# Transformer block on one core: the order of key-value root, key transposes and query sums around the last Strassen pair

## The chip, the cores and the metric

One core of a Trainium2 chip runs the whole program. The metric is device time in microseconds, the median of three runs. The core has five engines, each with its own instruction queue that it works through in order: PE (TensorE: matmuls and transposes), DVE (VectorE), ACT (ScalarE), POOL (GpSimd) and SP (SyncE, which here only issues DMAs). They meet through semaphores.

## The reference, cut to what matters

The layer is a residual block: a recurrent branch and a latent attention branch, mixed by gates, then a mixture of experts. Only the latent attention's entrance matters here. 1024 tokens, width 1024, query latents of 768, key-value latents of 256, 16 heads:

```
proj = u @ w_in                       # u = rms_norm(h); holds q_c, kv_c, k_pe among others
q  = (rms_norm(q_c, q_a_g) @ w_uq)    # 768 -> 16 heads x 96
kv = (rms_norm(kv_c, kv_a_g) @ w_ukv) # 256 -> 16 heads x (64 + 64): k_nope, v
k  = concat(k_nope, k_pe)             # k_pe, 32 wide, is the same for all heads
q  = rms_norm(q, q_norm_g); k = rms_norm(k, k_norm_g)
rope on the last 32 of q and k; chunk-causal softmax(q k^T / sqrt(96)) v
```

The norms of the latents need, for each token, the sum of squares over all features of the latent, and one over its root. The kernel applies that factor late, to values, to the sums of keys and queries, and divides the rotated key part by it.

## The kernel before, in words

Tokens lie along the free dimension in the projection: a latent tile is 128 features by 1024 tokens. Weights and activations are split into a high and a low part and multiplied three times, so that the result is near full precision. `pair(c0, ...)` (L227) computes two feature tiles by one level of Strassen: 7 products of 12 matmuls with 512 columns each, 84 in all. Its two weight tiles come through the raw tiles s0, s1, s2 in turn (`raw_tile`).

The stage in question runs in this order as written: the pair of the key-value latents (`latents(C_KV)`), their scaled high and low parts ckh and ckl (L620, L621), the rotation of the shared key part (L623 to L629), the last pair, which is the fifth and sixth tile of the query latents (`latents(C_Q + 4 * P)`), then the key-value sums over features (`token_sums(sk)`: 8 matmuls against a column of ones into pss), the root (`inverse`: L614 and the small DVE operations L80 to L92, into rkv), its reciprocal and its product with kpeR (L633, L634), the scaled query latents written to c_d (L636, L637), eight transposes of kpeR (ptk, L642), and the sums and root of the query latents (ss4, rq). After that comes `keys` (L705) and `values` (L764) for eight pairs of heads, two by two with the weights ukv of a group, while ACT and DVE split the query latents read back from c_d into cqh and cql (L1057, L96).

The order on each engine is not the order of the text. The program is written for a framework that places instructions in each engine's queue by when its own model has them ready, and keeps a tile's reuse safe by waits. Tiles of a pool come free when their last reader is done; the region of the activations (pool up) is released behind the last pair, and the tiles s9 and above lie in it, c_d's readings among them.

```
h = 0; r.append(raw_tile()...); nc.sync.dma_start(r[h], w_in_v[...])   # pair: weights
pss[:, i:i+1] = sq[:, i*P:(i+1)*P].T @ ones[:, :1]                      # token_sums, 8 times
st = raw_tile(); nc.sync.dma_start(st, w_ukv[...]); split(wh, wl, st)    # load_ukv
```

Of the kernel before, what the change touches and what calls it, by code (L numbers as in the profile page):

```python
# [10 lines left out]
F32 = mybir.dt.float32  # L11
# [3 lines left out]
AF = mybir.ActivationFunctionType  # L15
OP = mybir.AluOpType
# [3 lines left out]
P = 128  # L20
T = 1024
D = 1024
NT = T // P
KD = D // P
QL, KVL = 768, 256
# [5 lines left out]
EPS = 1e-6  # L31
# [7 lines left out]
def block_kernel(ctx: ExitStack, tc, a, out):  # L39
    nc = tc.nc  # L40
# [32 lines left out]
    def rsqrt(dst, src, shape, pool):  # L73

        n = int(np.prod(shape))
        view = lambda t: t if len(shape) == 1 else t.rearrange("p (a b) -> p a b", a=shape[0])
        gi = pool.tile([P, n], I32, tag=f"rsi{n}", name="rs_i")
        tt = pool.tile([P, n], F32, tag=f"rst{n}", name="rs_t")
        g3, t, y = view(gi), view(tt), view(gi.bitcast(F32))
        V.tensor_scalar(g3, src.bitcast(I32), 1, -1, op0=OP.arith_shift_right, op1=OP.bitwise_xor)  # L80
        V.tensor_tensor(gi, gi, magic[:, :n], op=OP.add)
        if n == 1:
            hs = pool.tile([P, 1], F32, tag="rsh", name="rs_h")
            V.tensor_scalar(hs, src, -0.5, None, op0=OP.mult)
            for it in range(3):
                V.scalar_tensor_tensor(t, y, y, hs, op0=OP.mult, op1=OP.mult)
                V.scalar_tensor_tensor(dst if it == 2 else y, t, 1.5, y, op0=OP.add, op1=OP.mult)
            return
        for it in range(3):
            V.tensor_tensor(t, y, y, op=OP.mult)  # L90
            V.scalar_tensor_tensor(t, t, -0.5, src, op0=OP.mult, op1=OP.mult)
            V.scalar_tensor_tensor(dst if it == 2 else y, t, 1.5, y, op0=OP.add, op1=OP.mult)  # L92
# [32 lines left out]
    def bank(nm="ps"):  # L125
        return bank2(nm)[:, 0] if psA is None else psA.tile([P, 512], F32, tag="ps", name=nm)
# [299 lines left out]
    def col(nm, k):  # L426
        return pcol[:, rows[nm] + k:rows[nm] + k + 1]
# [41 lines left out]
        V.tensor_scalar(hbx, pcol[:, rows["lru_bx"]:rows["lru_bx"] + 8], 0.5, None, op0=OP.mult)  # L469


    def token_sums(sq):

        pss = bank("pss")
        for i in range(NT):
            TE.matmul(pss[:, i:i + 1], sq[:, i * P:(i + 1) * P], ones[:, :1], start=True, stop=True)
        return pss[:, :NT]
# [119 lines left out]
    lk = tc.alloc_tile_pool(name="lk", bufs=1, side="right", reuse_waits="tile")  # L597
    ckh = lk.tile([P, 2, T], F32R, name="ckh")
    ckl = lk.tile([P, 2, T], F32R, name="ckl")
    with tc.tile_pool(name="wB", bufs=2, side="right", reuse_waits="tile") as wB:  # L600

        def latents(c0):
            t = wB.tile([P, 2, T], F32, tag="o", name="o")
            o = [t[:, j] for j in range(2)]
            pair(c0, o, S.copy)
            sacc, sq = (wB.tile([P, T], F32, tag=nm, name=nm, bufs=1) for nm in ("sacc", "sq"))
            S.activation(sacc, o[0], AF.Square)
            S.activation(sq, o[1], AF.Square)
            V.tensor_tensor(sacc, sacc, sq, op=OP.add)
            return o, sacc  # L610

        def inverse(dst, pss, n):
            sr = wB.tile([P, NT], F32, tag="sr", name="sr")
            V.tensor_scalar(sr, pss, 1.0 / n, EPS, op0=OP.mult, op1=OP.add)  # L614
            rsqrt(dst, sr, [NT], wB)

        o, sk = latents(C_KV)
        for j in range(2):
            g1 = col("kv_a_g", j)
            S.activation(ckh[:, j], o[j], AF.Copy, scale=g1)  # L620
            V.scalar_tensor_tensor(ckl[:, j], o[j], g1, ckh[:, j].bitcast(F32), op0=OP.mult, op1=OP.subtract)  # L621
        ksq = wB.tile([P, NT, DR], F32, name="ksq", bufs=1)
        S.activation(ksq, kp, AF.Square)  # L623
        V.tensor_reduce(sspe, ksq, axis=AX.X, op=OP.add)
        t1 = wB.tile([P, NT, DR], F32, name="t1", bufs=1)
        V.tensor_tensor(kpeR, kp, tC[:, 1], op=OP.mult)
        V.tensor_tensor(t1[:, :, :16], kp[:, :, 16:], tS[:, 1, :, :16], op=OP.mult)
        V.tensor_tensor(t1[:, :, 16:], kp[:, :, :16], tS[:, 1, :, 16:], op=OP.mult)
        V.tensor_tensor(kpeR, kpeR, t1, op=OP.add)  # L629
        oq, sq_ = latents(C_Q + 4 * P)  # L630
        inverse(rkv, token_sums(sk), KVL)
        rec = wB.tile([P, NT], F32, name="rec", bufs=1)
        V.reciprocal(rec, rkv)  # L633
        V.tensor_tensor(kpeR, kpeR, rec.unsqueeze(2).to_broadcast([P, NT, DR]), op=OP.mult)  # L634
        for j in range(2):
            S.activation(oq[j], oq[j], AF.Copy, scale=col("q_a_g", 4 + j))  # L636
            nc.gpsimd.dma_start(c_d[(4 + j) * P:(5 + j) * P, :], oq[j])  # L637
        kpT = wB.tile([P, T], F32, tag="sq", name="kpT", bufs=1)
        for hf in range(2):
            pt = bank("ptk").rearrange("p (c t) -> p c t", c=4)  # L640
            for i in range(4):
                TE.transpose(pt[:DR, i], kpeR[:, 4 * hf + i], ident)  # L642
            V.tensor_copy(kpT[:DR, hf * 512:(hf + 1) * 512].rearrange("p (i t) -> p i t", i=4), pt[:DR])
        nc.gpsimd.dma_start(pe_d, kpT[:DR])
        V.tensor_tensor(ss4, ss4, token_sums(sq_), op=OP.add)
        inverse(rq, ss4, QL)
    up.release()
    psA.release()
    psA = None
# [23 lines left out]
    def side_bank(nm):  # L673
        return psW.tile([P, 2, 512], F32, tag="po", name=nm, bufs=1)
# [22 lines left out]
    def keys(pp, wC):  # L697

        wh, wl = ukv[pp // 2]
        c = slice(pp % 2 * P, pp % 2 * P + P)  # L700
        ps = bank2("pk")
        for hf in range(2):
            for k in range(2):
                for n, (l, r) in enumerate(((wh, ckh), (wh, ckl), (wl, ckh))):
                    TE.matmul(ps[:, hf], l[:, 0, k, c], r[:, k, hf * 512:(hf + 1) * 512],  # L705
                              start=(k == 0 and n == 0), stop=(k == 1 and n == 2))
        ps = ps.rearrange("p h t -> p (h t)")
        kt = wC.tile([P, T], F32, tag="kt", name="kt")
        sq = new(17 + pp)
        S.activation(sq, ps, AF.Square)  # L710
        S.activation(kt, ps, AF.Copy, scale=col("k_norm_g", 0))
        nc.gpsimd.dma_start(k_d[pp * P:(pp + 1) * P, :], kt)
        sqs.append(sq)
        run_late()
        if pp % 4 == 3:
            late.append(lambda: sums(pp // 4))
# [343 lines left out]
    with tc.tile_pool(name="wC", bufs=2, side="right", reuse_waits="tile") as wC:  # L1060
        for g in range(4):
            keys(2 * g, wC)
            if g < 3:
                ukv[g + 1] = load_ukv(g + 1)
            else:
                uq[0] = load_uq(0)
            values(g, 0, wC)
            keys(2 * g + 1, wC)
            values(g, 1, wC)
# [524 lines left out]
```

## Time and profile before

| | |
|---|---|
| median of three runs | 1420.1 us (1417.18 to 1422.19) |
| profiled execution, its own time | 1418.82 us |
| its span, first to last instruction | 1417.1 us |
| mean granted clock of PE, share of full | 0.979 |
| busy PE, DVE, ACT, POOL | 1344.1, 1090.0, 783.0, 382.0 us |
| chain that ended last | PE 83%, DVE 11%, DMA 2%, ACT 2% |

All times below are microseconds from the span's start in the profiled execution. A row of a timeline gives start, duration, engine, line and operation, and in brackets how long the engine had been idle before and what released it. PEclk is the granted clock as a share of 2.4 GHz; 0.5 is 1.2 GHz.

### The profile page before, as it was taken

The numbers are of one execution on the slowest core, as the hardware profiler recorded it, in microseconds if no ns is written. First come the engines' busy times: TensorE is split into PE (matmuls) and PEld (weight loads), VectorE is DVE, ScalarE is ACT, GpSimd is POOL, SyncE is SP. The second block draws the span as 40 slices with busy tenths as digits, with TensorE's granted clock in tenths as the row PEclk, the third lists the DMA queues.
The fourth block names the chain that finished last, engine by engine and source line by source line (L and its number), as shares of the span: only waits on it lengthen the run. The fifth ranks groups of instructions, "written<-read, shape, count | busy, mean of one in ns | idle before, by whom it ended". The sixth has DMA issues, their size and how long they took to land.

```text
span 1417.1 us, 20382 instructions
## 1 busy us (share of the span) xinstructions
PE 1344.1 (95%) x7371; PEld 1094.3 (77%) x7372; DVE 1090.0 (77%) x1894; ACT 783.0 (55%) x1138; POOL 382.0 (27%) x313
## 2 busy tenths in 40 slices
PE   5999999999999899998999999998995999999995
PEld 4967888888888788987655555557874999999995
DVE  7698878787966655678577777785496899999894
ACT  5444747565734353423444444444532888888884
POOL 2100000000000211221777777550422222222222
PEclk9999999999999899999999999999997999999998
DMA  6112222222353545643434444363567899999962
GB/s 216 49 59 87 89 75 89 75 90 89 134 178 120 178 173 172 174 148 99 116 100 117 107 120 132 107 220 134 198 233 250 289 379 381 380 380 379 368 175 36
DMA packets 119945, 244.32 MB, mean 172 GB/s; under 512 B 32636, under 2 KB 68564, under 8 KB 119840
## 3 DMA queue, kind: packets, MB, share of 16 engines
q1 hardware_dynamic: 101768, 194.37, 40.9%
q0 software_dynamic: 17616, 48.46, 11.1%
q8 instruction: 59, 0.97, 0.3%
q14 instruction: 46, 0.38, 0.1%
q10 hardware_dynamic: 456, 0.14, 0.0%
HBM read 203.87 MB, written 55.83 MB: 183 GB/s over the span
## 4 chain that ended last, share of the span: by engine, by line
PE 83%; DVE 11%; DMA 2%; ACT 2%; issue 1%; POOL 0%; SPq 0%; POOLq 0%; DVEq 0%; ACTq 0%
PE pw L245 22%; PE pg L1442 13%; PE po L971 6%; PE py L1479 6%; PE pq L787 6%; PE ph L1172 4%; PE psm L923 3%; PE psl L560 3%; PE pss L953 3%; PE pss L955 2%; PE pss L954 2%; PE pt L1424 2%; PE pp L164 2%; PE pk L705 2%; PE pv L764 1%; DVE s L96 1%
## 5 line engine op out<-in xcount | busy, mean ns | idle before, releaser
L96 ACT CAST s<-s 128x1024 fp32r<-128x1024 f32 (+4 forms) x392 | 337.9, 882 | 179.8 <-PE pw L245 39.7
L96 DVE TENSOR_TENSOR s<-s,s 128x1024 fp32r<-128x1024 f32 (+3 forms) x384 | 382.5, 1023 | 52.8 <-ACT s L96 47.4
L1442 PE MATMUL pg<-s,s 128*128 128x256 f32 x1536 | 196.3, 284 | 0.7 <-DVE s L96 0.7
L1442 PEld LDWEIGHTS pg<-s,s 128*128 128x128 f32 x1536 | 189.8, 191 | 3.5 <-DVE s L96 0.9
L245 PE MATMUL pw<-uh,s 128*128 128x512 f32 x576 | 183.0, 392 | 0.0
L956 ACT ACTIVATE s<-pss 128x512 f32<-128x512 f32 (+4 forms) x192 | 90.1, 493 | 148.6 <-PE pss L955 144.9
L976 POOL TENSOR_TENSOR s<-s,s 128x896 f32<-128x896 f32 (+6 forms) x108 | 149.8, 1406 | 58.3 <-ACT s L956 40.8
L245 PEld LDWEIGHTS pw<-uh,s 128*128 128x128 f32 x576 | 108.8, 189 | 23.9 <-ACT s L96 0.9
L924 DVE TENSOR_REDUCE mx<-psm 128x1 f32<-128x320 f32 (+4 forms) x192 | 94.5, 547 | 41.1 <-PE psm L923 40.7
L245 PE MATMUL pw<-ul,s 128*128 128x512 f32 x288 | 112.7, 391 | 0.0
L971 PE MATMUL po<-s,s 128*64 128x512 f32 (+3 forms) x384 | 106.8, 507 | 0.3 <-ACT s L956 0.3
L1172 PE MATMUL ph<-s,s 128*128 128x512 f32 x384 | 98.3, 404 | 3.5 <-ACT s L96 2.9
L787 PE MATMUL pq<-s,cqh 128*128 128x384 f32 x384 | 99.2, 337 | 0.0
L1479 PE MATMUL py<-s,hT 128*128 128x512 f32 x384 | 96.2, 399 | 1.2 <-ACT hT L96 1.2
L1485 POOL DMA_INDIRECT out_dram<-s,idx x32 | 54.7, 1709 | 121.6 <-ACT s L1484 107.4
L1172 PEld LDWEIGHTS ph<-s,s 128*128 128x128 f32 x384 | 70.6, 191 | 19.5 <-ACT s L96 4.1
L1479 PEld LDWEIGHTS py<-s,hT 128*128 128x128 f32 x384 | 69.8, 188 | 15.1 <-ACT hT L96 1.4
L953 PE MATMUL pss<-s,s 128*128 128x512 f32 (+4 forms) x192 | 72.9, 380 | 3.0 <-ACT s L956 3.0
L1416 POOL DMA_INDIRECT s<-xs,idx x32 | 35.7, 1117 | 131.2 <-PE pt L1424 107.1
L953 PEld LDWEIGHTS pss<-s,s 128*128 128x128 f32 x192 | 36.4, 189 | 44.0 <-DVE mx L924 17.0
L787 PEld LDWEIGHTS pq<-s,cqh 128*128 128x128 f32 x384 | 69.2, 188 | 1.1 <-DVE vt L768 0.8
L955 PE MATMUL pss<-s,s 128*128 128x512 f32 (+4 forms) x192 | 65.8, 343 | 0.0
(389 smaller groups left out, 2603.8 us busy)
## 6 DMA issues: line engine op xcount, KB each, us to landing
s<-in_w_gate_dram SPq DMA_DIRECT2D x64, 512.0 KB
s<-in_w_up_dram SPq DMA_DIRECT2D x63, 512.0 KB
s<-in_w_down_dram SPq DMA_DIRECT2D x63, 512.0 KB
s<-in_w_in_dram SPq DMA_DIRECT2D x40, 512.0 KB
s<-rk_d SPq DMA_DIRECT2D x16, 384.0 KB
q_d<-qt POOLq DMA_DIRECT2D x8, 768.0 KB, 4.7
s<-q_d SPq DMA_DIRECT2D x16, 384.0 KB
s<-in_w_uq_dram SPq DMA_DIRECT2D x12, 384.0 KB
```

The source lines that it names most:

```text
L96: return S.copy(hi, src), by.tensor_tensor(lo, src, hi.bitcast(F32), op=OP.subtract)
L245: TE.matmul(ps[at], w[:, l, k], ub[b][m][:, k], start=(go and k == 0 and n == 0), stop=(k == K4 - 1 and n == 2), skip_group_check=True)
L787: TE.matmul(p2[:, t % 2, :384], l[:, k, i * P:(i + 1) * P], wq[k // 2][r][:, k % 2], start=(k == 0 and n == 0), stop=(k == 5 and n == 2))
L924: V.tensor_reduce((mx[:, j, R1 + i:R1 + i + 1], mx2[:, j, i:i + 1])[b], ps[:, :cn], axis=AX.X, op=OP.max, negate=True)
L953: TE.matmul(o[:, :cn], kh[:, ks], qh[:, q], start=True, stop=False)
L955: TE.matmul(o[:, :cn], kh[:, ks], ql[:, q], start=False, stop=True)
L956: S.activation(pT[:, b * cn:(b + 1) * cn], o[:, :cn], AF.Exp)
L971: TE.matmul(po[pp][s][j * DV:(j + 1) * DV, lo - s * 512:], va[:, c, j, :], pTs[j][:, lo - c * P:hi - c * P], start=(c == 0), stop=(c == 4 ...
L976: (V if pp == NP - 1 and j == 0 and c < 5 else G).tensor_tensor(ac, ac, pTs[j][:, :T - c * P], op=OP.add)
L1172: TE.matmul(o, m2[l][:, k], wo[c][k // 2][r][:, k % 2], start=(k == 0 and m == 0), stop=(k == KD - 1 and m == 2))
L1442: TE.matmul(pg[:, u], l[:, k], r, start=(k == 0 and m == 0), stop=(k == KD - 1 and m == 2))
L1479: TE.matmul(py[hf], l[:, k, :], wd[k][w][:, hf * 512:(hf + 1) * 512], start=(k == 0 and m == 0), stop=(k == 1 and m == 2))
```

## The change

`inverse` is moved out of the stage's pool and takes a pool as an argument. The key-value sums, the root, the product with kpeR, the eight transposes and the write to pe_d are now written ahead of the last pair. The sums of squares of the two pairs no longer share a tile: the key-value ones get a tile of their own (sk), the query ones a raw tile (saq). The sums and the root of the query latents are written into the loop over keys and values, behind `keys(0)`, with a side bank of PSUM as their target.

```
--- before.py
+++ after.py
@@ -469,9 +469,9 @@
         V.tensor_scalar(hbx, pcol[:, rows["lru_bx"]:rows["lru_bx"] + 8], 0.5, None, op0=OP.mult)
 
 
-    def token_sums(sq):
-
-        pss = bank("pss")
+    def token_sums(sq, pss=None):
+
+        pss = bank("pss") if pss is None else pss
         for i in range(NT):
             TE.matmul(pss[:, i:i + 1], sq[:, i * P:(i + 1) * P], ones[:, :1], start=True, stop=True)
         return pss[:, :NT]
@@ -597,24 +597,25 @@
     lk = tc.alloc_tile_pool(name="lk", bufs=1, side="right", reuse_waits="tile")
     ckh = lk.tile([P, 2, T], F32R, name="ckh")
     ckl = lk.tile([P, 2, T], F32R, name="ckl")
+
+    def inverse(dst, pss, n, pool):
+        sr = pool.tile([P, NT], F32, tag="sr", name="sr")
+        V.tensor_scalar(sr, pss, 1.0 / n, EPS, op0=OP.mult, op1=OP.add)
+        rsqrt(dst, sr, [NT], pool)
+
     with tc.tile_pool(name="wB", bufs=2, side="right", reuse_waits="tile") as wB:
 
-        def latents(c0):
+        def latents(c0, sums):
             t = wB.tile([P, 2, T], F32, tag="o", name="o")
             o = [t[:, j] for j in range(2)]
             pair(c0, o, S.copy)
-            sacc, sq = (wB.tile([P, T], F32, tag=nm, name=nm, bufs=1) for nm in ("sacc", "sq"))
+            sacc, sq = sums(), wB.tile([P, T], F32, tag="sq", name="sq", bufs=1)
             S.activation(sacc, o[0], AF.Square)
             S.activation(sq, o[1], AF.Square)
             V.tensor_tensor(sacc, sacc, sq, op=OP.add)
             return o, sacc
 
-        def inverse(dst, pss, n):
-            sr = wB.tile([P, NT], F32, tag="sr", name="sr")
-            V.tensor_scalar(sr, pss, 1.0 / n, EPS, op0=OP.mult, op1=OP.add)
-            rsqrt(dst, sr, [NT], wB)
-
-        o, sk = latents(C_KV)
+        o, sk = latents(C_KV, lambda: wB.tile([P, T], F32, name="sk", bufs=1))
         for j in range(2):
             g1 = col("kv_a_g", j)
             S.activation(ckh[:, j], o[j], AF.Copy, scale=g1)
@@ -627,14 +628,10 @@
         V.tensor_tensor(t1[:, :, :16], kp[:, :, 16:], tS[:, 1, :, :16], op=OP.mult)
         V.tensor_tensor(t1[:, :, 16:], kp[:, :, :16], tS[:, 1, :, 16:], op=OP.mult)
         V.tensor_tensor(kpeR, kpeR, t1, op=OP.add)
-        oq, sq_ = latents(C_Q + 4 * P)
-        inverse(rkv, token_sums(sk), KVL)
+        inverse(rkv, token_sums(sk), KVL, wB)
         rec = wB.tile([P, NT], F32, name="rec", bufs=1)
         V.reciprocal(rec, rkv)
         V.tensor_tensor(kpeR, kpeR, rec.unsqueeze(2).to_broadcast([P, NT, DR]), op=OP.mult)
-        for j in range(2):
-            S.activation(oq[j], oq[j], AF.Copy, scale=col("q_a_g", 4 + j))
-            nc.gpsimd.dma_start(c_d[(4 + j) * P:(5 + j) * P, :], oq[j])
         kpT = wB.tile([P, T], F32, tag="sq", name="kpT", bufs=1)
         for hf in range(2):
             pt = bank("ptk").rearrange("p (c t) -> p c t", c=4)
@@ -642,8 +639,10 @@
                 TE.transpose(pt[:DR, i], kpeR[:, 4 * hf + i], ident)
             V.tensor_copy(kpT[:DR, hf * 512:(hf + 1) * 512].rearrange("p (i t) -> p i t", i=4), pt[:DR])
         nc.gpsimd.dma_start(pe_d, kpT[:DR])
-        V.tensor_tensor(ss4, ss4, token_sums(sq_), op=OP.add)
-        inverse(rq, ss4, QL)
+        oq, saq = latents(C_Q + 4 * P, raw_tile)
+        for j in range(2):
+            S.activation(oq[j], oq[j], AF.Copy, scale=col("q_a_g", 4 + j))
+            nc.gpsimd.dma_start(c_d[(4 + j) * P:(5 + j) * P, :], oq[j])
     up.release()
     psA.release()
     psA = None
@@ -1060,6 +1059,9 @@
     with tc.tile_pool(name="wC", bufs=2, side="right", reuse_waits="tile") as wC:
         for g in range(4):
             keys(2 * g, wC)
+            if g == 0:
+                V.tensor_tensor(ss4, ss4, token_sums(saq, side_bank("pss")[:, 0]), op=OP.add)
+                inverse(rq, ss4, QL, wC)
             if g < 3:
                 ukv[g + 1] = load_ukv(g + 1)
             else:
```

On PE, between the two pairs, before: pw_3647 is the last product of the key-value pair, pw_3757 the first of the last pair (uh, ul: high and low part of the activations; s: weight tiles).

```order
L245 MATMUL pw_3647<-ul1_115,s5_3713 128x512
L245 MATMUL pw_3647<-uh1_113,s5_3713 128x512
L245 MATMUL pw_3757<-uh0_112,s6_3754 128x512
L245 MATMUL pw_3757<-ul0_114,s6_3754 128x512
L245 MATMUL pw_3757<-uh0_112,s6_3754 128x512 x2
L245 MATMUL pw_3757<-ul0_114,s6_3754 128x512
```

The last pair follows the key-value pair directly. The same place in the changed kernel (pw_3798 is now the first product of the last pair, pss the key-value sums, ptk the transposes):

```order
L245 MATMUL pw_3647<-ul1_115,s5_3713 128x512
L245 MATMUL pw_3647<-uh1_113,s5_3713 128x512
L476 MATMUL pss_3746<-ones_80,sk_3729 128x1 x8
L639 MATMUL ptk_3774<-ident_72,kpeR_710 32x128 x4
L639 MATMUL ptk_3780<-ident_72,kpeR_710 32x128 x4
L245 MATMUL pw_3798<-uh0_112,s6_3795 128x512
L245 MATMUL pw_3798<-ul0_114,s6_3795 128x512
```

The sums and the transposes have moved in front of all matmuls of the last pair. On PE behind the last pair, before (pk: keys, sacc: the sums of squares of the two pairs):

```order
L245 MATMUL pw_3791<-uh1_113,s7_3857 128x512
L476 MATMUL pss_3878<-ones_80,sacc_3729 128x1 x8
L642 MATMUL ptk_3910<-ident_72,kpeR_710 32x128 x4
L642 MATMUL ptk_3916<-ident_72,kpeR_710 32x128 x4
L476 MATMUL pss_3923<-ones_80,sacc_3873 128x1 x8
L705 MATMUL pk_4074<-ckh_3597,s3_4041 128x512
L705 MATMUL pk_4074<-ckl_3598,s3_4041 128x512
L705 MATMUL pk_4074<-ckh_3597,s8_4042 128x512
```

Behind the last product stand key-value sums, transposes, query sums and then the keys. The same place in the changed kernel (s1 holds the sums of squares of the query latents, s3 and s8 the weights ukv of group 0, high and low, pv the values):

```order
L245 MATMUL pw_3832<-uh1_113,s7_3898 128x512
L476 MATMUL pss_4067<-ones_80,s1_3914 128x1 x8
L704 MATMUL pk_4049<-ckh_3597,s3_4016 128x512
L704 MATMUL pk_4049<-ckl_3598,s3_4016 128x512
L763 MATMUL pv_4101<-s3_4016,ckh_3597 128x256
L704 MATMUL pk_4131<-ckh_3597,s3_4016 128x512
L704 MATMUL pk_4049<-ckh_3597,s8_4017 128x512
L704 MATMUL pk_4049<-ckh_3597,s3_4016 128x512
```

Only the query sums are left there, still ahead of the first key matmul; four matmuls that don't need s8 come next. On SP around the first reading of c_d, before (s0, s1: raw tiles for ukv, s11 and above: query latents):

```order
L678 DMA s1_4092<-in_w_ukv_dram 128x2x512
L678 DMA s0_4039<-in_w_ukv_dram 128x2x512
L678 DMA s0_4198<-in_w_ukv_dram 128x2x512
L678 DMA s1_4313<-in_w_ukv_dram 128x2x512
L1057 DMA s11_4047<-c_d_70 128x1024
L1057 DMA s12_4051<-c_d_70 128x1024
L1057 DMA s13_4055<-c_d_70 128x1024
L1057 DMA s14_4059<-c_d_70 128x1024
L1057 DMA s16_4067<-c_d_70 128x1024
L1057 DMA s15_4063<-c_d_70 128x1024
```

All four ukv loads are issued ahead of the c_d readings; s0_4039 is the one of group 0. In the changed kernel:

```order
L677 DMA s0_4092<-in_w_ukv_dram 128x2x512
L677 DMA s0_4313<-in_w_ukv_dram 128x2x512
L1056 DMA s11_4022<-c_d_70 128x1024
L1056 DMA s12_4026<-c_d_70 128x1024
L1056 DMA s13_4030<-c_d_70 128x1024
L677 DMA s1_4014<-in_w_ukv_dram 128x2x512
L1056 DMA s14_4034<-c_d_70 128x1024
L1056 DMA s15_4038<-c_d_70 128x1024
L1056 DMA s16_4042<-c_d_70 128x1024
L677 DMA s1_4198<-in_w_ukv_dram 128x2x512
```

The load of group 0 (s1_4014, in the tile that holds the query sums of squares) now stands behind three c_d readings, that of group 2 behind all six.

In DVE's queue the low part of group 0's weights, s8, was made in the course of the last pair; now it stands behind the root of the query latents and two of the six splits cql.

## Rows read from the trace of the kernel before

**Rows 1.** The page's chain that ended last, share of the span by engine

```profile
PE 83%; DVE 11%; DMA 2%; ACT 2%; issue 1%; POOL 0%; SPq 0%; POOLq 0%; DVEq 0%; ACTq 0%
```

**Rows 2.** PE in order of time, 480 to 494 (start us, us, operation)

```profile
480.19 1.84 PE L476 MATMUL pss<-ones,sacc 128*128 128x1 f32 x16
...
487.99 1.89 PE L642 MATMUL ptk<-ident,kpeR 128*32 128x128 f32 x8 [5.97 <-DVE kpeR L634]
...
489.67 3.41 PE L476 MATMUL pss<-ones,sacc 128*128 128x1 f32 x16
...
492.95 0.77 PE L705 MATMUL pk<-ckh,s 128*128 128x512 f32 x1
```

**Rows 3.** Stretches (us, busy by engine, PEclk, DMA share, GB/s)

```profile
482.10:487.95 5.85, 0.00 (x0) 0.00 (x0) 5.50 (x17) 2.17 (x2) 2.15 (x3) 0.58 0.95 366
...
493.05:496.70 3.65, 3.65 (x10) 2.88 (x10) 2.17 (x13) 0.00 (x0) 0.00 (x0) 0.50 0.60 197
...
505.50:546.00 40.50, 40.50 (x270) 34.09 (x270) 19.99 (x42) 19.22 (x21) 9.70 (x15) 1.00 0.66 232
```

**Rows 4.** PE inside the keys

```profile
505.48 0.39 PE L764 MATMUL pv<-s,ckh 128*128 128x256 f32 x1 [1.23 <-ACT kt L711]
```

**Rows 5.** DVE in order of time, 461 to 467

```profile
461.35 0.69 DVE L272 TENSOR_TENSOR o<-pw,o 128x512 f32<-128x512 f32 x1 [1.33 <-PE pw L245]
...
463.22 1.23 DVE L609 TENSOR_TENSOR sacc<-sacc,sq 128x1024 f32<-128x1024 f32 x1
...
466.76 0.68 DVE L268 TENSOR_TENSOR s<-s,s 128x512 f32<-128x512 f32 x1
```

**Rows 6.** DVE in order of time, 482 to 485

```profile
482.06 0.17 DVE L614 TENSOR_SCALAR sr<-pss 128x8 f32<-128x8 f32 x1 [0.98 <-PE pss L476]
...
482.75 1.00 DVE L80 TENSOR_SCALAR rs_i<-sr 128x8 int32<-128x8 int32 x1
...
484.54 1.22 DVE L609 TENSOR_TENSOR sacc<-sacc,sq 128x1024 f32<-128x1024 f32 x1
```

**Rows 7.** POOL in order of time, at three places

```profile
468.59 1.98 POOL L844 TENSOR_SCALAR_AFFINE_SELECT s<-s 128x512 f32<-128x512 f32 x3
...
482.32 1.42 POOL L851 TENSOR_SCALAR_AFFINE_SELECT s<-s 128x1024 f32<-128x1024 f32 x1
...
635.86 2.38 POOL L887 TENSOR_TENSOR s<-s,s 96x1024 f32<-96x1024 f32 x1 [0.36 <-DMA s<-pe_d]
```

**Rows 8.** DVE at 636

```profile
636.10 2.18 DVE L92 SCALAR_TENSOR_TENSOR rs_i<-rs_t,rs_i 128x32 f32<-128x32 f32 x1
```

**Rows 9.** DVE in order of time, behind the last pair

```profile
480.39 0.69 DVE L272 TENSOR_TENSOR o<-pw,o 128x512 f32<-128x512 f32 x1 [2.03 <-PE pw L245]
...
493.12 0.16 DVE L645 TENSOR_TENSOR ss<-ss,pss 128x8 f32<-128x8 f32 x1 [2.52 <-PE pss L476]
...
493.52 0.17 DVE L80 TENSOR_SCALAR rs_i<-sr 128x8 int32<-128x8 int32 x1
...
499.70 6.91 DVE L96 TENSOR_TENSOR cql<-s,cqh 128x1024 fp32r<-128x1024 f32 x6 [4.00 <-ACT cqh L96]
```

**Rows 10.** PE in order of time, 664 to 668

```profile
664.25 0.77 PE L953 MATMUL pss<-s,s 128*128 128x512 f32 x1 [3.00 <-ACT s L956]
...
667.37 0.39 PE L954 MATMUL pss<-s,s 128*128 128x512 f32 x1
```

**Rows 11.** ACT in order of time

```profile
472.50 2.19 ACT L96 CAST s<-s 128x512 fp32r<-128x512 f32 x4 [4.40 <-DMA s<-in_w_ukv_dram]
...
482.06 1.06 ACT L607 ACTIVATE sacc<-o 128x1024 f32<-128x1024 f32 x1 [0.34 <-PE pss L476]
```

**Rows 12.** The queue of SP, an earlier ukv load

```profile
468.85 0.37 SPq L678 DMA_DIRECT2D s<-in_w_ukv_dram  x1
```

**Rows 13.** DMA issues, 440 to 512 (count, size, us to landing)

```profile
c_d<-o POOLq DMA_DIRECT2D x2, 512.0 KB, 6.9
```

More of the change, by code (lines that the diff above doesn't have):

```diff
@@ L469, in decay_consts, with token_sums @@
         V.tensor_scalar(hbx, pcol[:, rows["lru_bx"]:rows["lru_bx"] + 8], 0.5, None, op0=OP.mult)
-    def token_sums(sq):
-        pss = bank("pss")
+    def token_sums(sq, pss=None):
+        pss = bank("pss") if pss is None else pss
         for i in range(NT):
@@ L599, in block_kernel, with inverse, latents @@
     ckl = lk.tile([P, 2, T], F32R, name="ckl")
+    def inverse(dst, pss, n, pool):
+        sr = pool.tile([P, NT], F32, tag="sr", name="sr")
+        V.tensor_scalar(sr, pss, 1.0 / n, EPS, op0=OP.mult, op1=OP.add)
+        rsqrt(dst, sr, [NT], pool)
     with tc.tile_pool(name="wB", bufs=2, side="right", reuse_waits="tile") as wB:
-        def latents(c0):
+        def latents(c0, sums):
             t = wB.tile([P, 2, T], F32, tag="o", name="o")
@@ L605, in latents @@
             pair(c0, o, S.copy)
-            sacc, sq = (wB.tile([P, T], F32, tag=nm, name=nm, bufs=1) for nm in ("sacc", "sq"))
+            sacc, sq = sums(), wB.tile([P, T], F32, tag="sq", name="sq", bufs=1)
             S.activation(sacc, o[0], AF.Square)
@@ L610, in latents @@
             return o, sacc
[L612 to L617, printed above, removed]
+        o, sk = latents(C_KV, lambda: wB.tile([P, T], F32, name="sk", bufs=1))
         for j in range(2):
@@ L629, in block_kernel @@
         V.tensor_tensor(kpeR, kpeR, t1, op=OP.add)
-        oq, sq_ = latents(C_Q + 4 * P)
-        inverse(rkv, token_sums(sk), KVL)
+        inverse(rkv, token_sums(sk), KVL, wB)
         rec = wB.tile([P, NT], F32, name="rec", bufs=1)
@@ L634, in block_kernel @@
         V.tensor_tensor(kpeR, kpeR, rec.unsqueeze(2).to_broadcast([P, NT, DR]), op=OP.mult)
-        for j in range(2):
-            S.activation(oq[j], oq[j], AF.Copy, scale=col("q_a_g", 4 + j))
-            nc.gpsimd.dma_start(c_d[(4 + j) * P:(5 + j) * P, :], oq[j])
         kpT = wB.tile([P, T], F32, tag="sq", name="kpT", bufs=1)
@@ L644, in block_kernel @@
         nc.gpsimd.dma_start(pe_d, kpT[:DR])
-        V.tensor_tensor(ss4, ss4, token_sums(sq_), op=OP.add)
-        inverse(rq, ss4, QL)
+        oq, saq = latents(C_Q + 4 * P, raw_tile)
+        for j in range(2):
+            S.activation(oq[j], oq[j], AF.Copy, scale=col("q_a_g", 4 + j))
+            nc.gpsimd.dma_start(c_d[(4 + j) * P:(5 + j) * P, :], oq[j])
     up.release()
@@ L1062, in block_kernel @@
             keys(2 * g, wC)
+            if g == 0:
+                V.tensor_tensor(ss4, ss4, token_sums(saq, side_bank("pss")[:, 0]), op=OP.add)
+                inverse(rq, ss4, QL, wC)
             if g < 3:
```

## The prediction, made before the changed kernel was run

> **What bounds the kernel now.** I read the chain of waits first, then the matmul engine in time where the chain leaves it, then the vector engine there. The chain lies on PE for 83% of the span and on DVE for 11% [rows 1]: the kernel ends sooner only where PE waits less. The change touches one place, from the end of the key-value pair to the first key block, so PE is read there row by row [rows 2]. The last pair ends at 480.19, where the key-value sums (pss) begin; they take 1.84 us. Then PE is idle for 5.97 us until DVE has finished kpeR. The eight transposes ptk (1.68 us to the start of what follows) and the query sums (3.41 us by their row) come next, and keys begin at 492.95: 12.76 us behind the last product. The granted clock is 0.58 in the idle stretch and 0.50 in the first 3.65 us of keys [rows 3], that is, mostly and then wholly at 1.2 instead of 2.4 GHz. One more idle of 1.23 us stands inside the keys, at 505.48 [rows 4].
>
> PE takes its instructions in order: the query sums' operand is ready at 485.76 (the addition of 484.54 takes 1.22 us, rows 6), yet their matmuls start at 489.67, behind the waiting transposes [rows 2]. So it matters in which order PE has them, and that order is printed above: in the changed kernel pss and ptk stand between the two pairs, ahead of all 84 matmuls of the last pair, and the query sums stand ahead of the first key matmul.
>
> **The change part by part.** All of it in the profiled execution's own times; that execution took 1418.82 us (span 1417.1), 1.3 below the median of 1420.1.
>
> *Between the pairs (new wait).* The last addition of a pair, L272, starts at 461.35 for the key-value pair and at 480.39 for the last one [rows 5, 9]; PE ends the last one 0.20 earlier, so the key-value pair ends at 461.15 and a pair is 19.04 us of PE. Nothing stops PE there now. In the changed kernel it waits for:
> (a) the sum of squares. DVE does L272 and one ckl product first and the addition L609 ends at 463.22 + 1.23 = 464.45 [rows 5]; that order is the same in the changed kernel. 3.3 us.
> (b) pss, 1.84 us before the clock fell and 3.41 at the lower one [rows 2]. The clock will fall somewhere around here, since PE has nothing for 3.3 us; I take the middle, 2.6.
> (c) DVE's chain. Before, it ran from 482.06 to 487.99, 5.93 us, but with the query latents' addition in it (484.54, 1.14 us of the chain), which is not there after, and with L80 at 1.00 us instead of 0.17 [rows 6, 9]. One split leaves it and L268 of the same length (0.68, rows 5) enters. 5.93 - 1.14 - 0.83 = 4.0 us.
> (d) GpSimd. L268 releases a memset and three selects on POOL; the selects take 1.98 us together and start 1.15 us behind the end of L268 (466.76 + 0.68; 468.59) [rows 5, 7]. Now the chain's small DVE operations, 0.20 apart, run beside them. Two rows show what that can cost: L80 ended with the select of 482.32 (1.42 us, to 483.74), and at 636.10 a small DVE operation took 2.18 us, until POOL's 2.38 us addition of 635.86 was over [rows 7, 8]. Five of the chain's operations go ahead of the selects. The ends are 0 and 1.9 us (all three selects waited out); by those two rows it is near the upper one, and I take 1.4, with one operation slipping through between two selects.
> The Trainium skill, "SBUF — State Buffer", section "Who interferes with whom", has the rule to it: a DVE instruction with two SBUF inputs contends with a GpSimd instruction that reads SBUF, not with one that only writes, and the later one waits for the whole of the other. The trace agrees with the first half (2.18 us); without the rule term (d) would be 0 and the forecast 1.4 lower.
> (e) ptk, 1.68 us as before, 0.85 if the clock had not fallen.
> Together 3.3 + 2.6 + 4.0 + 1.4 + 1.7 = 13.0 us, ends 10.0 and 15.1 (L80 held again, 0.8).
> (f) Clock. The last pair then starts at 1.2 GHz. Behind an idle of 3.00 us at 664.25 matmuls were slow until 667.37, 3.1 us [rows 10]; at the keys 3.65 [rows 3]. Half of that is lost: 1.8 us, ends 1.55 and 3.65 (two such stretches).
> The last pair ends 14.8 us later than before. What waits behind PE there (the splits for its later products) is ready, so nothing is won back inside the pair; ukv for group 1 lands some 12 us into it, ahead of its use.
>
> *Behind the last pair.* Removed: pss of the keys, the wait for kpeR, ptk. What is late next: the query latents' squares. L272 ends 0.9 us behind the last product [rows 9], the square takes 1.06 [rows 11], the addition 1.23: 3.2 us. It used to lie beside the DVE chain; nothing covers it now. PE waits, because the query sums stand ahead of keys: 2.6 us, as in (b), to 5.8. And the sums now sit in s1, the tile into which the weights ukv of group 0 are loaded, so this load is issued only when PE has read them, behind three loads of c_d on SP. An earlier ukv load went out at 468.85 and its cast started at 472.50 [rows 11, 12], 3.65 us: 9.5, cast 10.1. The third key matmul also needs the low part from DVE, and there the inverse root (thirteen operations 0.20 apart, as from 493.12 on, 2.6 us) and two cql splits of 1.15 (6.91 for six) stand ahead [rows 9]: 5.8 + 2.6 + 2.3 + 0.7 = 11.4 us. Before, the third key matmul stood 1.0 us behind the first, at 13.76. Four matmuls have slipped ahead, two of them of later blocks (0.3 us). Gain 2.6 us; ends: 3.4 gained if the sums take 1.84, 0.6 lost if the load lands only 6.9 us after issue, as the c_d transfers did [rows 13], since it shares the engines with these.
>
> *Inside the keys.* The idle of 1.23 us came from ACT, busy with six cqh casts before kt; two to six of them are now done ahead of the first key block. I take -1.2, ends -1.2 and 0. The clock: as low as before, perhaps for one stretch longer, +0.5 (0 to 1.8).
>
> The rest of the edits (other tiles, a side bank, kpT's write to pe_d earlier on POOL) I cost at nothing: pe_d is read behind the loads of uq, far from here, and from 505.5 to 546 PE is busy for all of 40.5 us [rows 3], so a transfer that is a little later there is hidden by the remaining keys; without that cover it would cost what it is late by.
>
> Sum: 13.0 + 1.8 - 2.6 - 1.2 + 0.5 = +11.5 us, 1430.3 against the profiled execution and 1431.5 against the median. All lower ends give +7, all upper ends +21.
>
> **Rivals.** *The tail is worth more than the front.* Place: behind the last pair. If neither the ukv load nor DVE's queue held keys there, they would start 5.0 us behind the last product (3.2 + 1.84) instead of 12.76, at full clock (1.8) and without the idle (1.2): -10.8. With the lower ends in front, 10.0 + 1.55 = 11.6, that is +0.8: 1420.9, not slower. For: with clock and idle the old tail is 15.8 us, more than the 14.8 of the new front. Against: the load into s1 can't be issued before PE has read s1, and 3.65 us of landing are in a row. It decides if keys start under 7 us behind the last product.
> *Everything at its worse end.* The selects hold the chain, the clock stays low for two stretches, and the load of group 0 lands among the c_d transfers: +18, 1438. For: DMA engines are 0.95 busy in the stretch behind the last pair before [rows 3]. Against: part of that traffic (two ukv loads) now lies elsewhere.
> *The change does not do what its order says:* PE passes over the waiting sums and runs the last pair. Then the front costs nothing and 2.6 + 1.2 are gained, 1416.3. Against it stands the second pss of rows 2, which did not pass ptk.
>
> **How the numbers follow.** Likeliest as summed: 0.74. All at its worse end: 0.14. Tail worth more than the front: 0.07. PE passing over: 0.05. A change of 0.3% (4.3 us) is about what can be told from none. Slower than that: 0.74 + 0.14 = 0.88; within: 0.07; faster: 0.05, since -3.8 is at the limit. The range 1425 to 1439 is that of the likeliest with most of the heavier case; the two cases below are left out.
>
> **What would show it.** Right: pss and ptk in front of the last pair, PE idle of about 3 and 5 us there with DVE named as releaser, the granted clock at 0.5 at the start of the last pair, its last product near 495, and keys waiting some 4 us behind the query sums for a cast or a DMA of in_w_ukv. Wrong: a last pair that starts before 470, keys under 7 us behind it, or the missing 1.23 us turning up later as another wait for vt or pv. The prediction is wrong altogether if PE's idle time between 461 and 506 is not longer than the 7.2 us of before.

## The result, and the profile after

| | median (range), runs | over before | ratio, 95% |
|---|---|---|---|
| before | 1420.28 us (1417.18 to 1422.19), 6 | | |
| after | 1433.42 us (1429.19 to 1436.04), 6 | +13.1 us | 1.0091 [1.0072, 1.0109] |
| predicted | 1431.5 us (1425 to 1439) | +11.5 us | |

The changed kernel is slower, and inside the range. Its profiled execution took 1436.04 us (span 1434.4, mean granted clock 0.970), 2.6 above its median, so the two profiles differ by 17.2 us.

The chain that ended last, on the page of after: DVE has grown from 11 to 13% [rows 1], DMA from 2 to 3%, at PE's expense.

```profile
PE 81%; DVE 13%; DMA 3%; ACT 1%; issue 1%; POOL 0%; SPq 0%; POOLq 0%; DVEq 0%; ACTq 0%
```

The same chain of after in order of time through the stage (start us, us, what; line numbers of after: L615 adds the squares, L622 is ckl, L603 to L92 the root, L639 the transposes):

```profile
461.33 0.17 DVE o L272
...
461.94 1.28 DVE ckl L622
463.22 1.22 DVE sk L615
...
464.48 3.59 PE pss L476 x16
...
470.89 0.52 DVE rs_t L90
471.41 0.02 issue
471.44 0.59 DVE rs_t L91
...
472.89 0.44 DVE kpeR L634
473.33 0.04 issue
473.37 1.89 PE ptk L639 x8
475.26 20.21 PE pw L245 x84
...
496.22 1.06 ACT s L613
497.28 0.02 issue
497.31 1.24 DVE s L615
...
498.59 3.58 PE pss L476 x16
502.19 4.51 DMA s<-in_w_ukv_dram
506.70 0.02 issue
506.72 0.63 ACT s L96
```

What to see: before, the chain stays on PE from the key-value pair into the last one. Now it leaves PE twice ahead of the last pair, once for the sum of squares and once for the root, and twice behind it, for the query squares and for the load of in_w_ukv into the tile where these lay. PE's own rows there (in brackets the idle time and its releaser) answer to rows 2:

```profile
464.48 3.58 PE L476 MATMUL pss<-ones,sk 128*128 128x1 f32 x16 [3.18 <-DVE sk L615]
473.37 1.89 PE L639 MATMUL ptk<-ident,kpeR 128*32 128x128 f32 x8 [5.32 <-DVE kpeR L634]
474.91 0.78 PE L245 MATMUL pw<-uh,s 128*128 128x512 f32 x1
...
498.59 3.57 PE L476 MATMUL pss<-ones,s 128*128 128x1 f32 x16 [3.13 <-DVE s L615]
...
507.39 0.80 PE L704 MATMUL pk<-ckh,s 128*128 128x512 f32 x1 [5.23 <-ACT s L96]
```

Idle time in this stretch is 16.9 us against 7.2 before [rows 2, 4]. The stretches of after (busy by engine, then PEclk, DMA share, GB/s) show the granted clock at 0.50, that is 1.2 GHz, in the sums, in the waits for kpeR and for the load, and at the start of the keys, and mostly so at the start of the last pair:

```profile
464.48:468.06 3.58, 3.57 (x16) 3.49 (x16) 1.14 (x1) 0.00 (x0) 0.00 (x0) 0.50 0.02 5
468.06:473.37 5.31, 0.00 (x0) 0.00 (x0) 4.85 (x16) 0.00 (x0) 2.85 (x4) 0.50 0.00 0
475.00:478.00 3.00, 3.00 (x10) 2.42 (x9) 0.80 (x2) 0.00 (x0) 0.56 (x1) 0.58 0.20 44
...
502.16:507.39 5.23, 0.00 (x1) 0.00 (x0) 4.55 (x16) 0.67 (x2) 0.00 (x0) 0.50 0.73 238
507.39:510.40 3.01, 3.01 (x8) 2.44 (x9) 2.83 (x4) 3.01 (x4) 0.00 (x0) 0.50 0.85 321
```

A ledger by first starts on PE (us; KV end is DVE's L272 behind the key-value pair, 0.2 us behind its last product):

| | before | after | difference so far |
|---|---|---|---|
| KV end | 461.35 | 461.33 | 0.0 |
| end of the last pair (L272) | 480.39 | 495.49 | +15.1 |
| first key product | 492.95 | 507.39 | +14.4 |
| first query product pq | 546.0 | 558.2 | +12.2 |
| first ph of the experts | 945.8 | 961.8 | +16.0 |
| end of the span | 1417.1 | 1434.4 | +17.3 |

So the touched stage costs 12.2 us, and queries and attention seem to cost 3.8 more. Below, "stage" is KV end to first pq (84.67 us before, 96.89 after), and "queries and attention" first pq to first ph, the first product of the experts (399.8 and 403.6).

### The profile page after: what moved, and what is told of

The parts are those of the page before. It is cut to its first block, busy times and chain, and to the rows that moved or that the text cites. A ratio compares the mean times of both kernels' runs of the same rounds, so it can differ in the third digit from the quotient of the medians.

```text
span 1434.4 us, 20375 instructions
## 1 busy us (share of the span) xinstructions
PE 1352.5 (94%) x7371; PEld 1100.8 (77%) x7372; DVE 1094.3 (76%) x1894; ACT 783.5 (55%) x1138; POOL 381.6 (27%) x313
## 4 chain that ended last, share of the span: by engine, by line
PE 81%; DVE 13%; DMA 3%; ACT 1%; issue 1%; POOL 0%; SPq 0%; POOLq 0%; DVEq 0%; ACTq 0%
PE pw L245 22%; PE pg L1444 13%; PE po L970 6%; PE py L1481 6%; PE pq L786 5%; PE ph L1174 4%; PE psm L922 3%; PE psl L560 3%; PE pss L952 3%; PE pss L954 2%; PE pss L953 2%; PE pt L1426 2%; PE pk L704 2%; PE pv L763 2%; PE pp L164 1%; DVE s L96 1%
## 5 line engine op out<-in xcount | busy, mean ns | idle before, releaser
L1481 PEld LDWEIGHTS py<-s,hT 128*128 128x128 f32 x384 | 69.8, 188 | 15.1 <-ACT hT L96 1.4
```

The source lines that it names most:

```text
L1481: TE.matmul(py[hf], l[:, k, :], wd[k][w][:, hf * 512:(hf + 1) * 512], start=(k == 0 and m == 0), stop=(k == 1 and m == 2))
```

## The experiments

Theory: PE waits in front of the last pair for two chains that used to lie beside it (the front), and what lies between the last pair and the keys (the tail) gives back little, since keys now wait for a load that the squares' tile holds up. Main rival: the front costs little, and the loss is the clock, the load, or later stages. A, B and C are the theories that each expectation names. Every time stands against runs of the kernel before on the same chip; stage, queries and attention are read from one profile each, and the two of after differ by 2.6 us in the last column.

| kernel | median, over before | ratio, 95% | stage, over before | queries and attention, over before |
|---|---|---|---|---|
| after (second profile) | 1433.42, +13.1 | [1.0072, 1.0109] | +12.2 (+12.0) | +3.8 (+1.2) |
| front_back | 1424.61, +5.0 | [1.0018, 1.0040] | +2.7 | +2.8 |
| mid_pair (second profile) | 1423.84, +4.3 | [1.0009, 1.0038] | -0.8 (+0.4) | +4.0 (+4.0) |
| squares_s2 | 1426.68, +7.1 | [1.0024, 1.0050] | +5.8 | +3.8 |
| mid_pair_s2 | 1411.80, -7.8 | [0.9924, 0.9958] | -9.0 | +1.7 |
| sums_front | 1430.42, +10.1 | [1.0047, 1.0091] | +8.4 | +4.9 |
| fill | 1431.73, +11.4 | [1.0069, 1.0100] | +8.6 | +4.7 |
| back_s2 | 1418.80, -1.5 | [0.9980, 1.0005] | -1.2 | +0.2 |
| mid_pair_dve | 1422.93, +2.9 | [1.0006, 1.0033] | +0.7 | +1.8 |
| mid_pair_s2_dve | 1411.63, -8.4 | [0.9924, 0.9954] | -9.0 | +0.4 |
| before, second profile | | | +0.2 | +0.3 |

**front_back: the front undone, the tail kept.** The call of the last pair moves ahead again of sums, root and transposes (cut; the writes to c_d move with it):

```diff
+        oq, saq = latents(C_Q + 4 * P, raw_tile)
         inverse(rkv, token_sums(sk), KVL, wB)
...
-        oq, saq = latents(C_Q + 4 * P, raw_tile)
```

> Only the front is undone: key-value sums, root and transposes stand behind the last pair again, all else as in the changed kernel (query sums' squares in the raw tile, sums and root of the query latents in the loop). Theory A (the 15 us between the pairs are the loss): PE has no gap between the pairs, the last pair ends within 1 us of 480.2, the time falls by about 10 us against the changed kernel, to 1421 to 1426; it stays 1 to 5 us over the kernel before, since keys now also wait for the load into the tile of the squares (4 us more behind the last product, 1.2 us of idle inside the keys gone). Rival B (the loss is the load and the slower stages behind it, and the front costs little): the time stays at 1430 or over. Rival C (the tail is a gain in itself): 1417 or under.

1424.61: A, at the upper part of its range. PE is not stopped between the pairs, and the last pair ends where it did before (its last product starts at 480.04). What is left, +2.7 us of stage, is the tail: keys start 18.1 us behind the last product, with the same 5 us wait for the cast of in_w_ukv. In the same profile queries and attention took 2.8 us more.

**sums_front: only sums and root in front.** `oq, saq = latents(...)` stands between the product with kpeR and the transposes.

> The front split in two: the key-value sums and the root stay ahead of the last pair, the transposes (and their wait for kpeR) stand behind it. Theory A (each wait between the pairs costs what its rows show): PE waits 3.2 us for the sum of squares and takes about 3.5 us for pss, then starts the last pair at half clock, ended near 488.5 to 489.5 instead of 495.3 (the 5.3 us wait for kpeR and 1.7 us of ptk gone from there); ptk comes behind the last product without a wait, so that the tail is no longer than in the changed kernel; 6 to 7 us less than the changed kernel, 1425 to 1428. Rival B (what counts is only that PE stops once between the pairs): within 2 us of the changed kernel, 1431 to 1435.

1430.42, over A's range. The front did nearly what A says: the last pair ends 5.5 us earlier, counted from KV end (28.6 us against 34.2), where A had 5.8 to 6.8, so each of the two waits has its own price. But the tail was 1.8 us longer than after's (first key product 13.9 us behind the last pair's end at 488.4, against 12.1), where I had said no longer: the query sums wait for the copies out of the transposes' bank, `[3.99 <-DVE kpT L644]`. And queries and attention lost 4.9 us (see the second profiles below).

**fill: useless products in the two gaps.**

```diff
-        inverse(rkv, token_sums(sk), KVL, wB)
+        idle = bank("idle")
+        for i in range(13):
+            TE.matmul(idle, ckh[:, 1, :P], ckh[:, 1, :512], start=True, stop=True)
+        kvs = token_sums(sk)
+        for i in range(4):
+            TE.matmul(idle, ones, sk[:, :512], start=True, stop=True)
+        inverse(rkv, kvs, KVL, wB)
```

> The changed kernel with work of no use in the two gaps between the pairs: 13 products of ckh (128x512) while PE would wait for the sum of squares, and four fp32 products of the squares with ones (128x512) while it would wait for kpeR; their result is not read. The waits stay as long, only the clock may differ. Theory A (the half clock behind each idle is a price of its own): pss takes 1.84 instead of 3.58 us, ptk about 1 instead of 1.7, the first product of the last pair runs at full clock (1.8 us), and the last product ends 3 to 4.5 us earlier, at 491 to 492.5; 1428.5 to 1431. Rival B (the pieces are bound by something other than the clock, or the gaps are not filled): pss stays at 3.5 us, the time within 1 us of the changed kernel or over it.

PE between the pairs in fill (columns as before):

```profile
460.72 3.25 PE L633 MATMUL idle<-ckh 128*128 128x512 f32 x13 [0.19 <-ACT ckh L621]
463.81 1.85 PE L476 MATMUL pss<-ones,sk 128*128 128x1 f32 x16
465.52 3.68 PE L636 MATMUL idle<-sk,ones 128*128 128x512 f32 x8
470.98 1.05 PE L645 MATMUL ptk<-ident,kpeR 128*32 128x128 f32 x8 [1.78 <-DVE kpeR L640]
```

The stretches of fill at the sums and behind the transposes (columns as above) show the granted clock at 1.00, where after has 0.50 and 0.58:

```profile
463.81:465.50 1.69, 1.69 (x17) 1.69 (x17) 1.05 (x1) 0.00 (x0) 0.00 (x0) 1.00 0.00 0
470.98:474.00 3.02, 3.02 (x18) 2.52 (x19) 1.28 (x2) 0.00 (x0) 0.56 (x1) 1.00 0.00 0
```

The waits are filled for the most part (1.78 us of idle are left), the sums take 1.85 instead of 3.58 us and the transposes 1.05 instead of 1.89. The last pair ends 3.6 us earlier, counted from KV end (30.6 us against 34.2). So 3.6 us of the front is clock, in the prediction's terms (b), (e) and (f). The time fell by 1.7 us only, 0.7 short of A's range; queries and attention took 4.7 us more than before's.

**squares_s2: the squares in a tile that nothing waits for.**

```diff
-        oq, saq = latents(C_Q + 4 * P, raw_tile)
+        oq, saq = latents(C_Q + 4 * P, lambda: new(2))
...
+        turn[0] += 1
```

The second line sends the first in_w_ukv to s1.

> As the changed kernel, but the query squares are summed in tile s2, which becomes free inside the last pair, and the first key-value weights go to s1, free before it; the zeroing and the three selects on GpSimd that use s2 come behind the query sums. PE's order then has the first key block ahead of the query sums. Theory A: the front stays (PE idle 3.2 and about 4 us between the pairs; the three slow operations of 0.5 us in DVE's root are back at 0.2, so 1.1 us less if it was the selects that held them); behind the last product keys start within 3 us instead of 12.1, at a higher clock; the query sums of 1.8 us come later in the stream. 8 to 11 us less than the changed kernel: 1422 to 1426. Rival B (keys wait for the cast or for DVE's queue and not for the load): keys still start 8 us or more behind the last product, 1430 or over. Rival C (the selects do not matter): the three operations stay at 0.5 us.

PE behind the last product in squares_s2:

```profile
492.40 0.39 PE L245 MATMUL pw<-uh,s 128*128 128x512 f32 x1
492.63 0.40 PE L705 MATMUL pk<-ckh,s 128*128 128x512 f32 x1
...
497.86 2.41 PE L476 MATMUL pss<-ones,s 128*128 128x1 f32 x16 [2.15 <-DVE s L615]
```

Keys follow the last product at once, where after has 12.1 us: the tail of after is the query sums and the load behind them. That is A's mechanism, but the time, 1426.68, is 0.7 us over its range: the stage gains 6.4 us and not 8 to 11, for one thing because the sums still stop PE behind the first key block (2.15 us idle, 2.41 us). C falls: with the selects moved away, the wait for kpeR is 4.16 instead of 5.32 us, and the last three operations of the root, 0.51, 0.57 and 0.58 us in after, take 0.17 each:

```profile
469.01 0.17 DVE L90 TENSOR_TENSOR rs_t<-rs_i 128x8 f32<-128x8 f32 x1
469.21 0.17 DVE L91 SCALAR_TENSOR_TENSOR rs_t<-rs_t,sr 128x8 f32<-128x8 f32 x1
469.41 0.17 DVE L92 SCALAR_TENSOR_TENSOR rkv<-rs_t,rs_i 128x8 f32<-128x8 f32 x1
```

**mid_pair: the sums behind the second product of the last pair, the transposes behind the fifth** (the expectation counts them as third and sixth). `pair` calls a function behind a product:

```diff
+            done[0] += 1
+            mid.get(done[0], lambda: None)()
...
-        oq, saq = latents(C_Q + 4 * P, raw_tile)
+        oq, saq = latents(C_Q + 4 * P, raw_tile, {2: root, 5: turned})
```

> As the changed kernel, but the key-value sums are asked for behind the third product of the last pair (by PE's order) and the transposes behind the sixth, so that PE has products to work on while ACT, DVE and the root run. Theory A: no PE gap over 0.5 us between 461 and the last product, pss 1.8 us and ptk about 0.9 us at full clock, the last pair ends near 483 instead of 495.3, the tail behind it as in the changed kernel (keys 12 us behind the last product); 12 us less than the changed kernel, 1419 to 1424, equal to the kernel before within 0.3%. Rival B (the time is not lost by waiting between the pairs, but by the clock that falls at any such spot, or later stages): less than 6 us gained, 1428 or over.

1423.84: A, near the upper end. PE has no idle time between 461 and the last product, pss takes 1.84 and ptk 1.03 us, the last pair ends at 482.4, and keys follow 11.7 us behind it.

**mid_pair_s2: mid_pair and squares_s2 together.**

> Both edits together: sums and transposes inside the last pair, and the query squares in s2 with the key-value weights loaded early. Theory A (the two waits are separate and their costs add): neither gap is left, keys start within 3 us of the last product, near 484 instead of 507.4 in the changed kernel and 492.95 in the kernel before; 1406 to 1412, that is 8 to 14 us under the kernel before. Rival B (what is won in this stage is given back later, because queries or attention then wait for transfers or for DVE): 1416 or over. Rival C (PE is bound by something else here and the time stands within 0.3% of the kernel before).

PE in mid_pair_s2, which has no idle time before these rows either:

```profile
464.65 1.84 PE L480 MATMUL pss<-ones,sk 128*128 128x1 f32 x16
474.66 1.03 PE L646 MATMUL ptk<-ident,kpeR 128*32 128x128 f32 x8
...
481.02 0.40 PE L713 MATMUL pk<-ckh,s 128*128 128x512 f32 x1
...
484.54 1.92 PE L480 MATMUL pss<-ones,s 128*128 128x1 f32 x16
```

The same 8 sums (16 matmuls in the trace) and 8 transposes, asked for two and five products later, cost 2.9 us of PE and no wait. mid_pair wins back 13.1 us of after's stage and 8.8 us of its time over before; between the second profiles it is 11.5 us in the stage less 2.9 us that queries and attention take longer, 8.7 together. In mid_pair_s2, with the load early as well, the stage is 9.0 us under before's and the kernel 7.8 us faster than before, in A's range. This is the version to keep.

**back_s2: the tail edit alone, sums as in the kernel before.** front_back with the two lines of squares_s2.

> Sums, root and transposes behind the last pair as in the kernel before, but the query squares in s2, the first key-value weights loaded early and the query sums in the loop (PE has them behind the first key block). The tail edit alone, with its load wait taken away. Theory A: PE is not stopped between the pairs; behind the last product pss 1.84, a wait of 5 us for kpeR, ptk 1.7, then keys at once, 9 us behind the last product instead of 12.76; with the idle of 1.2 us in keys gone and the query sums of 1.8 us put into the stream, 2 to 4 us under the kernel before, 1415.5 to 1418. Rival B (the wait for kpeR is covered by keys since nothing they need is late): 1410 to 1413, as the version with the sums inside the pair, so that the move ahead of the pair has no use at all. Rival C (queries and attention give it back): 1419 or over.

1418.80, not to be told from before. Its mechanism is A's (ptk `[5.97 <-DVE kpeR L635]`, first key product at 487.70, 9.4 us behind the last pair's end), its time 0.8 us over A's range. B falls: the early load does not by itself put keys into the wait for kpeR, since the transposes stand ahead of them. So moving the sums forward is worth some 6 us, if they go into the pair and not ahead of it.

**after_again, before_again, mid_pair_again: does the later loss belong to the kernels?**

> The changed kernel once more, for a second profile. Behind the stage (first query product to the first matmul ph of the experts) its first profile took 403.6 us, 3.8 us more than that of the kernel before (399.8). If that belongs to the change, the second profile shows 402.5 us or more there; if it is scatter between executions, it comes out anywhere between 399 and 404.

> The kernel before once more, for a second profile: from the first query product to the first ph its first profile took 399.8 us. If what the other kernels lose there (400.0 to 404.7) is scatter, this profile comes out between 399 and 404; if it belongs to their changes, at 400.5 or less.

> The version with the sums inside the last pair once more, for a second profile. Its stage was 0.8 us shorter than before's and its median 4.3 us longer; its first profile lost 4.0 us between the first query product and the first ph (403.8 against 399.8), with PE idle for 1.95 and 1.27 us at 605 to 608 and a stretch of half clock behind it. If that is a property of the kernel (transfers or DVE late at the entrance of attention), both come back at the same place, 402.8 us or more; if scatter, one of them is missing or the stretch comes out under 402.

before 399.8 and 400.1, mid_pair 403.8 twice with both idles back: there it belongs to the kernel. after 403.6 and 401.0: by the expectation's own line (402.5) that counts as scatter, and only 0.9 us lies over both profiles of before. The rows say more. In both profiles of after, and in neither of before, PE waits some 150 us behind the first query product for one small DVE operation beside a row of GpSimd's products. POOL, DVE and PE of after:

```profile
702.47 5.90 POOL L975 TENSOR_TENSOR s<-s,s 128x640 f32<-128x640 f32 x5
704.56 3.83 DVE L926 TENSOR_TENSOR mx<-mx,mx 128x8 f32<-128x8 f32 x1
708.45 0.43 PE L929 MATMUL ptm<-ident,mx 128*112 128x128 f32 x2 [2.04 <-DVE mx L926]
```

DVE and PE of before at the same place:

```profile
692.15 0.48 DVE L927 TENSOR_TENSOR mx<-mx,mx 128x8 f32<-128x8 f32 x1
693.93 0.43 PE L930 MATMUL ptm<-ident,mx 128*112 128x128 f32 x2
```

In all fourteen profiles this operation goes with the stretch: it lasts 3.50 to 3.83 us in the ten with 401.0 to 404.7 us, and 0.16 to 0.88 us in the four with 399.8 to 400.1 (both of before, back_s2, mid_pair_s2_dve). So part of the later loss seems to come with after as well; no run takes the hold away from after alone, so this rests on the rows. Its size stays open: behind the wait the granted clock was 0.50 from 710.3 to 713.0 in the first profile of after and 1.00 all along in the second. That 12.0 + 1.2 = 13.2 in the second profile meets the 13.1 between the medians is partly chance: its span is 14.7 us over before's, with 1.2 less ahead of the stage and 2.7 more behind the first ph, where before's own two profiles differ by 2.2.

The same mechanism is seen most clearly in sums_front, at the entrance of attention, where after itself loses nothing (PE waits 1.31 and 0.71 us there, 0.97 and 1.03 in before). First POOL, then DVE, then PE:

```profile
612.05 2.37 POOL L886 TENSOR_TENSOR s<-s,s 96x1024 f32<-96x1024 f32 x1 [12.05 <-DMA s<-rk_d]
614.36 0.79 POOL L806 DMA_DIRECT2D q_d<-qt  x1
615.17 1.50 POOL L879 TENSOR_TENSOR s<-s,scq 128x768 f32<-128x768 f32 x1
```

```profile
612.11 4.61 DVE L90 TENSOR_TENSOR rs_t<-rs_i 128x32 f32<-128x32 f32 x1
616.65 0.68 DVE L923 TENSOR_REDUCE mx<-psm 128x1 f32<-128x512 f32 x1
```

```profile
617.38 0.79 PE L922 MATMUL psm<-s,s 104*128 104x512 f32 x1 [4.20 <-DVE mx L923]
```

A DVE operation of 0.2 us starts 0.06 us behind GpSimd's and ends with the second one; the reduction queued behind it is late, and PE waits 4.20 us for it. In the kernel before, GpSimd has L887 behind the write of q_d, where it meets the root later.

**mid_pair_dve, mid_pair_s2_dve: that product of the second head on DVE.**

```diff
-            G.tensor_tensor(t[:DQ], t[:DQ], bc[:DQ], op=OP.mult)
+            (V if (pp, j) == (0, 1) else G).tensor_tensor(t[:DQ], t[:DQ], bc[:DQ], op=OP.mult)
```

> The version with the sums inside the last pair, and one product of 96x1024 at the entrance of attention (the second head's key part times its scale) on DVE instead of GpSimd. In both profiles of that version GpSimd has this product ahead of the write of q_d (behind it in the kernel before), it takes 2.36 us, and DVE's small operation beside it 2.38; PE waits 1.95 and 1.05 to 1.27 us there and runs at half clock for 6.8 us. Theory A (this hold is what the version gives back): the small operation is 0.2 us again, DVE pays about 1.2 us for the product itself, PE's two waits fall to 1 us or less together and the half clock stretch goes; from the first query product to the first ph 400 to 402 us instead of 403.8; 1.5 to 4 us less, 1420 to 1422.5. Rival B (DVE is then late by the product itself, or the loss lies elsewhere): within 1 us of 1423.8 or over.

> The best version so far (sums inside the pair, query squares in s2, 1411.8) with the same product on DVE. There GpSimd's product of 2.44 us held small DVE operations for 1.66 and 1.35 us, and PE waited 1.27 us. Theory A: those operations are 0.2 us again, the wait falls to 0.5 us or less; 0.5 to 2 us less, 1409.8 to 1411.3. Rival B: no change within 0.5 us, or slower, since DVE does 1.2 us more.

By their times both go with rival B: they moved by 0.9 and 0.2 us, less than their runs scatter. Queries and attention fell by 2.2 and 1.3 us, in mid_pair_dve into A's range, and PE's two waits there from 3.2 to 1.95 us, where A had 1 or less; but another product of 96x1024 took the place on GpSimd (2.40 us) and still holds L91 for 1.66 us. In mid_pair_s2_dve the operations at the entrance stayed held (1.70 and 1.48 us); what went is the later hold, 0.88 instead of 3.70 us for the operation on mx. That the hold takes time from PE is shown; how much of the later loss it is, is not.

## Why the prediction was right

Step by step, in the profiled execution:

| term | predicted | measured | where |
|---|---|---|---|
| (a) sum of squares | 3.3 | 3.35 | 461.13 to 464.48 |
| (b) pss | 2.6 | 3.58 | its row |
| (c) + (d) root, with the selects | 5.4 | 5.31, of it 1.16 the selects | idle row; squares_s2 |
| (e) ptk | 1.7 | 1.54 | 473.37 to 474.91 |
| (f) half clock in the last pair | 1.8 | 1.34 | 474.91 to 495.29, less 19.04 |
| front | 14.8 | 15.1 | ledger |
| tail | -2.6 | -0.7 | first key product 12.1 us behind the last one, 12.76 before |
| keys | -0.7 | -2.2 | first key product to pq, 50.8 instead of 53.1 |
| tail and keys | -3.3 | -2.9 | ledger, 12.2 less 15.1 |
| stage | +11.5 | +12.2 | ledger |

The front was right in its mechanism, and in size in each term but (b): I took the middle between the two rows of pss, and the clock had fallen before the sums began (0.50 for the whole of their row). fill, at 1.00, shows the clock to be the cause. (e) and (f) came out 0.2 and 0.5 us lower, so that the sum of the front is off by 0.3 only. (d) came out at 1.16 instead of 1.4, and by another picture: not one operation slips through between two selects while the rest waits, but each of three operations waits one select of 0.63 us out.

In the tail the mechanism was right (query squares 3.3 us, sums, load, cast, all in the chain), and two sizes were off: the sums again 3.57 instead of 2.6, and the load 4.5 instead of 3.65, at a DMA share of 0.73 in that stretch. I had let DVE's queue decide the third key product, behind the load's 10.1; in fact DVE was through with the root and the two cql splits at 507.17 and waited 0.20 us for the cast, so both chains ended together. The first key product came 12.1 us behind the last one of the pair. The third one, which needs s8, is the fifth in PE's order now; it started at 509.05, 1.66 us later at half clock. That is 13.8 us behind the last one, as before (13.76), where I had 11.4. With the two products of later blocks ahead of it (0.64 us) the tail gained 0.65 us instead of 2.6.

The keys gave that back: from the first key product to pq they took 50.8 instead of 53.1 us, where I had counted 0.7 less. 1.23 us of it is the idle of rows 4, which is gone as predicted and did not turn up later as a wait of pv. The other 1.0 us I did not have: it lies in the sums over the keys, ssp. Before, two of their 32 matmuls stand alone at 503.20, ahead of that idle, and take 1.04 us, besides two groups of 1.92 us; in after all 32 run in two groups of 1.92 us. So the tail was 1.9 us worse and the keys 1.5 us better than taken, and that their sum is off by 0.4 only is luck.

Of the rivals, the tail worth more than the front needed keys within 7 us; they came at 12.1. Its price of -10.8 was of the right size all the same: where the load doesn't hold keys up, the stage less the front comes to -8.5 us in squares_s2 and -11.7 in mid_pair_s2. What the prediction put at nothing is everything behind the keys: it asked only whether a later transfer would be covered, and what came is a DVE operation beside another row of GpSimd's work, part of the 3.8 and 1.2 us of the two profiles of after.

## What to carry to other kernels

An in-order engine pays for an instruction where it stands, not where its result is needed: before moving a small product ahead of a long block, add up the chain that feeds it from the end of the previous block, and put it that many products into the block. Look at what tile an early result sits in: the next load into that tile starts when the result has been read. And a moved edit changes the order on engines far away; compare stage by stage, with a second profile, before blaming the stage that was touched.

## What the runs showed of the hardware

A small DVE operation can last as long as the GpSimd work beside it: one of 128x32 (0.19 us alone) took 4.61 us in sums_front, across two products and a DMA issue on GpSimd, and one of 128x8 (0.16 us in back_s2) took 3.83 us in after, beside a row of products. The Trainium skill, "SBUF — State Buffer", section "Who interferes with whom", says that a DVE instruction with two SBUF inputs contends with a GpSimd instruction that reads SBUF and not with one that only writes. The traces agree: beside the memset of 469.69 to 470.64 in after the root's operations took 0.17 us each, beside the selects 0.51 to 0.58.

An idle of 3.2 us cost PE more than itself: the granted clock was 0.50 for the 3.58 us of sums behind it and the 5.31 us wait, and 0.58 in the first 3 us of products. Kept busy with useless products (fill), PE had 1.00 there, the same sums took 1.85 us, and the transposes 1.05 instead of 1.89.
